# Where partial sums are kept and when a gate's norm is taken: two re-orderings in a hybrid convolution and state-space layer

## The chip, the core and the metric

The kernel runs on one core of a Trainium2 chip. The metric is the device time of one execution in microseconds (us); every kernel is run several times and the median counts. The core has a matrix engine (TensorE, PE in the profile), a vector engine (VectorE, DVE), a scalar engine (ScalarE, ACT), a general engine (GpSimd, POOL) and a queue that starts transfers (SyncE, SP). Each engine takes its own instructions strictly in the order in which they stand, and waits where a semaphore has not come. PE writes its sums to PSUM, from which ACT and DVE read.

## The reference

One layer of a diffusion backbone, on 256 positions of a prompt and 1024 of a sample that share all weights. The part that matters here:

```python
proj = h @ w_in                                  # D = 1024 -> 3072 columns
hc, gb, gc, z, xbc, dtf, dtb = split(proj)
out_a = gb * dwconv1d(gc * hc, w_conv_short)     # short convolution, gated
xbc = silu(dwconv1d(xbc, w_conv_ssd, b_conv_ssd))
dt_f, dt_b = softplus(dtf + dt_bias[0]), softplus(dtb + dt_bias[1])
y = y_f + y_b_rev[:, ::-1] + xh * d_skip         # two chunked scans, chunks of 128
y = rmsnorm(y * silu(z), g_ssd_norm)             # the gate and its norm
out = concatenate([out_a, y]) @ w_out
```

Then follow a second norm and a gated feed-forward block with a 3x3 convolution, which the change does not touch. Everything is in float32.

## The kernel before

A float32 operand is split into two numbers of half the digits, hi and lo, and a product is three matmuls: hi by hi, hi by lo and lo by hi (lines 160, 162 and 164 in `mm3`). Channels lie on the 128 partitions, positions along the free dimension. One **projection** makes 128 columns of `proj` for one set: 8 tiles of the inner dimension by 3 matmuls, so 24 matmuls of 128x256 for the prompt, and 48 of 128x512 for the sample (two chunks of 512).

Each projection loads its weights anew (`wload`, line 146): a transfer, ACT's rounding to hi (line 151), and the subtraction that gives lo (`tt`, line 77), on POOL or on DVE as the caller says (`PG`, `PV`). Every third set of weights goes to the tiles `whx` and `wlx`, of which there is one each; the others to `whi` and `wlo`, of which there are two. So ACT's rounding for a later projection waits until PE is done with the earlier one that used the same tile.

The accumulators are PSUM tiles: `acc` (two of 128x1024), `sa` (three of 128x512) and `yp` (one). `proj_halves` takes an `sa` for the first two projections of the prompt and a whole `acc` for each later one, though a projection of the prompt fills only 256 of its 1024 columns. The counter `s.n` numbers a set's projections from 1.

The prompt's 24 projections run in this order: eight of `xbc` (n = 1 to 8; `i` is 0 to 7; readers ACT at line 396 and two DVE operations at line 80, the convolution), four of `zproj` (z0 to z3, n = 9 to 12; reader ACT at line 409, whose result a transfer of ACT's queue writes away), then `outa` four times (n = 13 to 24). `outa` makes three projections: hc (reader ACT, line 423), gc (reader DVE, a product; then ACT at line 431 and two DVE operations of the convolution), and gb (reader DVE, a product; then ACT at line 440 and a DVE subtraction). Beside them runs `dtstage`, the step sizes: one small matmul (line 458), then a chain that alternates between ACT (lines 461 to 502) and DVE (lines 468 to 498). `dttok` transposes its result on PE (lines 513 and 523; before the last one DVE makes `dg`, line 520).

The sample's projections follow, and then the state-space part. `ssd_pass2` runs over the chunks in units (two to a chunk, one for each group of heads): `front` makes a chunk's transposes and products, `prep` the decay matrices, `output` the 12 or 8 small matmuls of y (line 657), and `fill` puts half a projection of the sample between them. The `gate` of a chunk is a generator of three steps: load z, then multiply and square (ACT and DVE), then the norm: two matmuls by a tile of ones (line 800), ACT's Ln and Exp (lines 804 and 805), and the product on DVE. `post_p` and `post_s` say behind which unit each step is issued. After the last unit the last chunk's norm is issued, and the rest of the fillers; then the gated result is split into hi and lo for the output projection (`mya`, `myb`).

The program's text is not the order on an engine: a scheduler places the instructions by their dependences and priorities, and `after` pins a few behind others. A tile is waited for as a whole: an instruction that writes one part of a tile waits for the readers of its other parts too.

Of the kernel before, what the change touches and what calls it, by code (L numbers as in the profile page):

```python
# [6 lines left out]
F32 = mybir.dt.float32  # L7
F32R = mybir.dt.float32r
AF = mybir.ActivationFunctionType
ALU = mybir.AluOpType  # L10
# [6 lines left out]
TP, TS = 256, 1024  # L17
# [11 lines left out]
TA = TP + RA * GW  # L29
# [26 lines left out]
def body(nc, tc, A):  # L56
    cnt = [0]

    def T(pool, shape, tag, bufs, dt=F32):
        cnt[0] += 1  # L60
        return pool.tile(list(shape), dt, tag=tag, bufs=bufs, name=f"{tag}_{cnt[0]}")
# [7 lines left out]
    def close_pool(g):  # L69
        g.__exit__(None, None, None)  # L70

    act = nc.scalar.activation
# [6 lines left out]
    def stt(out, a, s, b, op0, op1):  # L79
        V.scalar_tensor_tensor(out=out, in0=a, scalar=s, in1=b, op0=op0, op1=op1)  # L80
# [14 lines left out]
    def smv(n):  # L95
        a, b = SMO[n]
        return sm[:, a:b]
# [29 lines left out]
    def pacc():  # L127
        return T(ps, [P, 1024], "acc", 2)
# [4 lines left out]
    def psa():  # L133
        return T(ps, [P, 512], "sa", 3)
# [11 lines left out]
    def wload(src, lo_eng, raw=None):  # L146
        if raw is None:
            raw = T(wst, [P, KT, P], "raw", 2)
        dma(raw, src)
        hi, lo = wpair()  # L150
        act(hi, raw, AF.Copy)  # L151
        tt(lo, raw, hi.bitcast(F32), ALU.subtract, lo_eng)
        return hi, lo

    def mm3(outs, wh, wl, n, ks=None):

        mms = []
        for k in ks or range(n):
            for o, rh, rl in outs:
                nc.tensor.matmul(o, wh[:, k, :], rh(k), start=k == 0, stop=False)  # L160
            for o, rh, rl in outs:
                nc.tensor.matmul(o, wh[:, k, :], rl(k), start=False, stop=False)  # L162
            for o, rh, rl in outs:
                mm = nc.tensor.matmul(o, wl[:, k, :], rh(k), start=False, stop=k == n - 1)  # L164
            mms.append(mm)
        return mms
# [108 lines left out]
    xq = T(xy, [P, 4, TS], "xs", 1)  # L275
# [34 lines left out]
    for k in range(KT):  # L310
# [7 lines left out]
        x = xs[k]  # L318
        tt(x, x, rs, ALU.mult)
        hi = T(hsp, [P, TS], "h", 16, F32R)  # L320
        act(hi, x, AF.Identity, scale=aff[:, 0, k, 1:2], bias=col(0, k, 1))
        ts(x, x, aff[:, 0, k, 1:2], col(0, k, 1), ALU.mult, ALU.add)
        lo = T(hsp, [P, TS], "h", 16, F32R)
# [10 lines left out]
        q, i = k // 4, k % 4  # L334
# [11 lines left out]
    for name, t0, n, v in (("p", 0, TP, 0), ("s", TP, TS, 1)):  # L346
        s = S()
# [11 lines left out]
    def proj(s, m, lo_eng):  # L359
        g = proj_halves(s, m, lo_eng)  # L360
        next(g)
        return next(g)

    def proj_halves(s, m, lo_eng):
        s.n += 1
        wh, wl = wload(A["w_in"][m], lo_eng, T(nrm, [P, KT, P], "x", 8) if s.name == "p" else None)
        pp = psa() if s.name == "p" and s.n <= 2 else pacc()
        outs = []
        for a, b in s.chunks:
            outs.append((pp[:, a:b], (lambda k, a=a, b=b: s.hi(k)[:, a:b]),  # L370
                         (lambda k, a=a, b=b: s.lo(k)[:, a:b])))
        ks = list(range(KT))
        for half in (ks[0:KT // 2], ks[KT // 2:]):
            ends = mm3(outs, wh, wl, KT, half)
            mid_mm[0] = ends[0]
            last_mm.append(ends[-1])
            yield pp[:, 0:s.T]
# [36 lines left out]
    def outa(s, j, lo_eng):  # L414

        n = s.T
        w = [smv("wcs")[:, j * 3 + t:j * 3 + t + 1] for t in range(3)]
        g = proj_halves(s, j, lo_eng)
        next(g)
        yield  # L420
        p1 = next(g)
        u = T(cv, [P, n], "cv", 4)
        act(u, p1, AF.Copy)
        yield
        g = proj_halves(s, 8 + j, lo_eng)
        next(g)
        yield
        p2 = next(g)
        tt(u, p2, u, ALU.mult)
        v = T(cv, [P, n], "cv", 4)  # L430
        act(v, u, AF.Copy, scale=w[1])
        conv1d_sb(v, u, w, n)
        yield
        g = proj_halves(s, 4 + j, lo_eng)
        next(g)
        yield
        p3 = next(g)
        tt(v, p3, v, ALU.mult)
        hi = T(cv, [P, n], "xl", 2, F32R)
        act(hi, v, AF.Copy)  # L440
        lo = T(cv, [P, n], "xl", 2, F32R)
        tt(lo, v, hi.bitcast(F32), ALU.subtract)
        dma(oad[j, 0, :, s.t0:s.t0 + n], hi.bitcast(F32))
        dma(oad[j, 1, :, s.t0:s.t0 + n], lo.bitcast(F32))
        yield
# [59 lines left out]
    def dttok(s, v, e2, ce):  # L505
        s.tok = T(sd, [P, s.nc, 2, 40], f"tok{s.name}", 1)
        for c0 in range(0, s.nc, 4):
            cn = min(4, s.nc - c0)
            tp = psa()
            for c in range(cn):  # L510
                for i, src in enumerate((v, e2)):
                    o = (c * 2 + i) * 40
                    mm = nc.tensor.transpose(tp[:, o:o + 40], src[:, (c0 + c) * L:(c0 + c + 1) * L],
                                             ident[0:40, 0:40])
                    if c0 == c == i == 0:
                        after(mm, last_mm[-1])
            act(s.tok[:, c0:c0 + cn].rearrange("p c i r -> p (c i r)"), tp[:, 0:cn * 80], AF.Copy)
        dg = T(cv, [40, 8, 40], "cv", 4)
        for i in range(s.nc):
            V.tensor_scalar(out=dg[:, i, :], in0=ident[0:40, 0:40], scalar1=ce[:, i:i + 1],  # L520
                            scalar2=None, op0=ALU.mult)
        pdx = psa()
        nc.tensor.matmul(pdx[:, 0:s.nc * 40], ones[0:40, :],
                         dg[:, 0:s.nc].rearrange("p c r -> p (c r)"), start=True, stop=True)
        s.dec = T(sd, [P, s.nc, 40], f"dec{s.name}", 1)
        s.last_exp = act(s.dec.rearrange("p c r -> p (c r)"), pdx[:, 0:s.nc * 40], AF.Exp)
# [164 lines left out]
    xall = T(xy, [P, 4, TP], "xp", 1)  # L691
# [23 lines left out]
    for j in range(4):  # L715
        for _ in outa(SP, j, PG):
            pass
        if j == 0:
            dttok(SP, *dts)
    dts = dtstage(SS, d4_s, silu)  # L720

# [31 lines left out]
    def fillers():  # L753
        for j in range(4):
            yield from zproj_halves(SS, j, PG)
        for j in range(4):
            yield from outa(SS, j, PG)

    filler = fillers()
# [26 lines left out]
    def gate(x, c0, n):  # L786

        z = T(cv, [P, 4, n], "cv", 4)
        for c in range(n // L):
            dma(z[:, :, c * L:(c + 1) * L], zd[c0 + c])  # L790
        yield
        if c0 == 0:
            act(z, z, AF.Silu)
        tt(x, x, z, ALU.mult)
        act(z, x, AF.Square)
        tt(z[:, 0:2], z[:, 0:2], z[:, 2:4], ALU.add)
        yield
        pp = psa()
        for i in range(2):
            mm = nc.tensor.matmul(pp[:, 0:n], ones, z[:, i], start=i == 0, stop=i == 1)  # L800
            if i == 0:
                after(mm, last_mm[-1])
        r = z[:, 2]
        act(r, pp[:, 0:n], AF.Ln, scale=1.0 / 512, bias=epsc)
        act(r, r, AF.Exp, scale=-0.5)
        tt(x, x, r.unsqueeze(1).broadcast_to([P, 4, n]), ALU.mult)
        yield

    gate_p = gate(xall, 0, TP)
    gates = [gate(xq[:, :, c * L:(c + 1) * L], SP.nc + c, L) for c in range(SS.nc)]  # L810
# [5 lines left out]
    def post_s(i):  # L816

        c = i // 2
        if i == 0:
            next(gate_p)  # L820
            next(gates[0])
        if i == 1:
            next(gate_p)
        if i % 2 == 1:
            next(gates[c])
        else:
            if c > 0:
                next(gates[c - 1])
            if c + 1 < SS.nc:
                next(gates[c + 1])  # L830

    ssd_pass2(SP, fill, post_p)
    ssd_pass2(SS, fill, post_s)
    with tc.high_priority():
        next(gates[-1])
    for _ in filler:
        pass
    close_pool(g_sw)
    close_pool(g_sd)

# [2 lines left out]
    g_yb, yb = open_pool("yb")  # L843
    mya = [[T(ya, [P, TA], "ya", 8, F32R) for _ in range(2)] for _ in range(4)]
    myb = [[T(yb, [P, OA], "yb", 8, F32R) for _ in range(2)] for _ in range(4)]
    with tc.high_priority():
        for x, dst, o in ((xall, mya, 0), (xq[:, :, 0:TA - TP], mya, TP), (xq[:, :, TA - TP:], myb, 0)):
            n = x.shape[2]
            for j in range(4):
                g = smv("gsd")[:, j:j + 1]  # L850
                hi, lo = [t[:, o:o + n] for t in dst[j]]
                act(hi, x[:, j], AF.Copy, scale=g)
                stt(lo, x[:, j], g, hi.bitcast(F32), ALU.mult, ALU.subtract)
    close_pool(g_xy)
    close_pool(g_cv)
    close_pool(g_hs)
# [386 lines left out]
```

## Time and profile before

| | |
|---|---|
| time, three runs | 1575.80, 1579.16 and 1581.37 us, median 1579.16 us |
| the profiled execution | 1580.42 us, of which the span on the core is 1578.5 us |
| granted PE clock, mean over the span | 0.991 of full speed |
| instructions of PE, DVE, ACT, POOL | 8722, 1634, 1025, 288 |

The profile is of one execution. "Busy" is the time in which an engine runs an instruction; for PE it includes time at half clock and matmuls that are stretched. A row of a timeline gives start, duration, engine, line and operation, tiles, shape, the count of instructions taken together, and in brackets the idle time ahead and what ended it. A row of a table of windows gives the window, its length, then busy time and instructions of PE, of its weight loads (PEld), of DVE, ACT and POOL, then the granted PE clock, the share of the transfer engines and GB/s. A row of the waits gives the waiting engine, tile and line, who was waited for, and us in all, how often, and the longest.

### The profile page before, as it was taken

What the parts mean: (1) busy time and instruction counts of PE and PEld (TensorE: products, weight loads), DVE (VectorE), ACT (ScalarE), POOL (GpSimd) and SP (SyncE); (2) the same over time, 40 slices, a digit from 0 to 9 for tenths busy, and PEclk for the clock granted to TensorE, in tenths of its full rate; (3) what the DMA queues carried; (4) which work ended last, traced back from release to release, by engine and by line L of the source; (5) the groups of instructions that cost most, each with busy time, mean ns of one, the idle gap of its engine ahead of it and who ended that gap; (6) DMA issues with size and microseconds to landing.
All of it is one profiled execution on the core that took longest, in us unless ns stands there. A gap on an engine that the chain in (4) does not pass through costs nothing. (4 is left out here: it accounts for less than half of the span.)

```text
span 1578.5 us, 22525 instructions
## 1 busy us (share of the span) xinstructions
PE 1525.0 (97%) x8722; PEld 1296.2 (82%) x8722; DVE 1101.3 (70%) x1634; ACT 662.0 (42%) x1025; POOL 513.8 (33%) x288
## 2 busy tenths in 40 slices
PE   6988999999999999999999999999999999999997
PEld 2688667777877888888888888888888888888886
DVE  5665615367787339797666598656679978798696
ACT  6553334257777235443332253332334433433333
POOL 1455001111110001343333333333346555445452
PEclk9999999999999999999999999999999999999999
DMA  8555554343434712322222233212252322343221
GB/s 304 214 184 162 216 202 147 111 150 123 144 101 146 286 67 82 112 73 69 66 68 78 66 133 112 70 65 67 76 184 93 102 99 99 106 161 97 93 78 61
DMA packets 86908, 191.98 MB, mean 122 GB/s; under 512 B 9330, under 2 KB 36626, under 8 KB 86802
## 3 DMA queue, kind: packets, MB, share of 16 engines
q1 hardware_dynamic: 80978, 187.41, 34.6%
q10 hardware_dynamic: 5824, 3.15, 0.7%
q8 instruction: 68, 1.11, 0.3%
q14 instruction: 38, 0.31, 0.1%
HBM read 167.37 MB, written 23.15 MB: 121 GB/s over the span
## 5 line engine op out<-in xcount | busy, mean ns | idle before, releaser
L80 DVE SCALAR_TENSOR_TENSOR cc<-acc,sm,cc 128x504 f32<-128x504 f32 (+5 forms) x836 | 545.7, 665 | 110.8 <-ACT cc L983 52.5
L77 POOL TENSOR_TENSOR wlo<-raw,whi 128x1024 fp32r<-128x1024 f32 (+2 forms) x83 | 193.5, 2331 | 672.4 <-ACT whi L151 518.5
L151 ACT ACTIVATE whi<-raw 128x1024 fp32r<-128x1024 f32 x90 | 95.1, 1057 | 243.6 <-PE acc L162 215.6
L80 DVE SCALAR_TENSOR_TENSOR x<-dn,mod,x 128x288 f32<-128x288 f32 (+2 forms) x176 | 96.1, 546 | 95.3 <-PE dn L164 95.1
L77 POOL TENSOR_TENSOR dlo<-draw,dhi 128x512 fp32r<-128x512 f32 (+1 forms) x88 | 108.9, 1238 | 90.8 <-ACT dhi L1036 88.8
L160 PE MATMUL acc<-ya,whi 128*128 128x512 f32 (+1 forms) x400 | 119.2, 355 | 1.4 <-DVE cv L77 1.4
L162 PE MATMUL acc<-ya,whi 128*128 128x512 f32 (+1 forms) x400 | 119.0, 355 | 0.0
L162 PE MATMUL acc<-oa,whi 128*128 128x512 f32 (+1 forms) x400 | 118.9, 355 | 0.0
L164 PE MATMUL acc<-ya,wlo 128*128 128x512 f32 (+1 forms) x400 | 118.7, 354 | 0.0
L164 PE MATMUL acc<-oa,wlo 128*128 128x512 f32 (+1 forms) x400 | 118.6, 354 | 0.0
L160 PE MATMUL acc<-oa,whi 128*128 128x512 f32 (+1 forms) x400 | 118.4, 353 | 0.0
L160 PE MATMUL dn<-yb,dhi 128*128 128x288 f32 (+2 forms) x352 | 110.0, 313 | 5.3 <-DVE x L80 4.1
L77 POOL TENSOR_TENSOR wlx<-raw,whx 128x1024 fp32r<-128x1024 f32 (+2 forms) x32 | 73.7, 2303 | 120.2 <-ACT whx L151 104.5
L162 PE MATMUL dn<-yb,dhi 128*128 128x288 f32 (+2 forms) x352 | 109.6, 311 | 0.8 <-POOL yb L77 0.8
L164 PE MATMUL dn<-yb,dlo 128*128 128x288 f32 (+2 forms) x352 | 109.6, 311 | 0.0
L160 PE MATMUL acc<-h,whi 128*128 128x512 f32 x320 | 105.7, 407 | 0.0
L1036 ACT ACTIVATE dhi<-draw 128x512 fp32r<-128x512 f32 (+1 forms) x88 | 52.9, 602 | 121.5 <-PE dn L162 50.8
L162 PE MATMUL acc<-h,whi 128*128 128x512 f32 x320 | 101.4, 396 | 0.0
L164 PE MATMUL acc<-h,wlo 128*128 128x512 f32 x320 | 100.8, 396 | 0.0
L160 PE MATMUL dn<-g,dhi 128*128 128x288 f32 (+2 forms) x304 | 95.1, 313 | 0.0
L162 PE MATMUL dn<-g,dhi 128*128 128x288 f32 (+2 forms) x304 | 94.8, 312 | 0.3 <-POOL g L77 0.3
L164 PE MATMUL dn<-g,dlo 128*128 128x288 f32 (+2 forms) x304 | 94.8, 312 | 0.0
(340 smaller groups left out, 3628.9 us busy)
## 6 DMA issues: line engine op xcount, KB each, us to landing
raw<-in_w_up SPq DMA_DIRECT2D x88, 512.0 KB, 3.2
x<-in_w_ada SPq DMA_DIRECT2D x32, 512.0 KB, 5.5
draw<-in_w_down SPq DMA_DIRECT2D x64, 256.0 KB, 2.7
x<-in_w_in SPq DMA_DIRECT2D x24, 512.0 KB, 3.3
raw<-in_w_in SPq DMA_DIRECT2D x22, 512.0 KB, 4.2
xs<-in_w_ad SPq DMA_DIRECT2D x16, 512.0 KB, 8.4
csb<-csds SPq DMA_DIRECT2D x16, 512.0 KB, 3.8
raw<-in_w_out SPq DMA_DIRECT2D x16, 512.0 KB, 3.2
```

What stands on the lines that cost most here:

```text
L77: (eng or V).tensor_tensor(out=out, in0=a, in1=b, op=op)
L80: V.scalar_tensor_tensor(out=out, in0=a, scalar=s, in1=b, op0=op0, op1=op1)
L151: act(hi, raw, AF.Copy)
L160: nc.tensor.matmul(o, wh[:, k, :], rh(k), start=k == 0, stop=False)
L162: nc.tensor.matmul(o, wh[:, k, :], rl(k), start=False, stop=False)
L164: mm = nc.tensor.matmul(o, wl[:, k, :], rh(k), start=False, stop=k == n - 1)
L1036: act(wh, raw, AF.Copy)
```

## The change

Three things. Prompt projections n = 3 and 4 share one `acc`, the second from column 512 on; so do 5 and 6, and so on to 23 and 24. The step sizes' transposes (`dttok`) are issued after the second `outa` and not after the first. And the gate's steps are issued later: a chunk's load and its norm behind odd units in place of even ones, the prompt's in another place, and the last chunk's norm inside the last projection of the sample, with the split of the first part written ahead of it.

```diff
     def proj_halves(s, m, lo_eng):
         s.n += 1
         wh, wl = wload(A["w_in"][m], lo_eng, T(nrm, [P, KT, P], "x", 8) if s.name == "p" else None)
-        pp = psa() if s.name == "p" and s.n <= 2 else pacc()
+        if s.name == "s":
+            pp = pacc()
+        elif s.n <= 2:
+            pp = psa()
+        else:
+            if s.n % 2:
+                s.acc = pacc()
+            pp = s.acc[:, 512 * (1 - s.n % 2):]
...
-        if j == 0:
+        if j == 1:
             dttok(SP, *dts)
...
         if i == 0:
-            next(gate_p)
             next(gates[0])
-        if i == 1:
-            next(gate_p)
         if i % 2 == 1:
             next(gates[c])
-        else:
             if c > 0:
                 next(gates[c - 1])
             if c + 1 < SS.nc:
                 next(gates[c + 1])
+        if i in (0, 3):
+            next(gate_p)
 
     ssd_pass2(SP, fill, post_p)
     ssd_pass2(SS, fill, post_s)
-    with tc.high_priority():
-        next(gates[-1])
-    for _ in filler:
-        pass
...
-    with tc.high_priority():
-        for x, dst, o in ((xall, mya, 0), (xq[:, :, 0:TA - TP], mya, TP), (xq[:, :, TA - TP:], myb, 0)):
-            n = x.shape[2]
-            for j in range(4):
-                g = smv("gsd")[:, j:j + 1]
-                hi, lo = [t[:, o:o + n] for t in dst[j]]
-                act(hi, x[:, j], AF.Copy, scale=g)
-                stt(lo, x[:, j], g, hi.bitcast(F32), ALU.mult, ALU.subtract)
+
+    def split(x, dst, o):
...
+    split(xall, mya, 0)
+    split(xq[:, :, 0:TA - TP], mya, TP)
+    next(filler)
+    next(filler)
+    next(gates[-1])
+    for _ in filler:
+        pass
+    split(xq[:, :, TA - TP:], myb, 0)
```

The new lines move the lines of the kernel behind them by 7 (409 becomes 416, 800 becomes 807).

**Place one: PE, from the prompt's gb0 to its hc1.** Before, the accumulators are `acc_1116` (gb0) and `acc_1168` (hc1); `sa_1149` and `sa_1158` are those of the step sizes' transposes. The 24 matmuls of gb0 stand together, and the transposes behind them:

```order
L162 MATMUL acc_1116<-bc_176,whi_1112 128x256
L164 MATMUL acc_1116<-bc_174,wlo_1113 128x256
L513 MATMUL sa_1149<-cst_66,cv_904 128x40 [waits DVE_49]
L513 MATMUL sa_1149<-cst_66,cv_909 128x40 [waits DVE_49]
L523 MATMUL sa_1158<-cv_1155,ones_70 128x80 [waits DVE_49,PE_49]
L160 MATMUL acc_1168<-bc_173,whx_1164 128x256
L162 MATMUL acc_1168<-bc_175,whx_1164 128x256
L164 MATMUL acc_1168<-bc_173,wlx_1165 128x256 [waits Pool_49]
```

Now gb0 and hc1 share `acc_1110`, and gc1 and gb1 share `acc_1180`; here gb0 ends, five matmuls of gc1 run, and hc1 starts:

```order
L162 MATMUL acc_1110<-bc_176,whi_1106 128x256
L164 MATMUL acc_1110<-bc_174,wlo_1107 128x256
L160 MATMUL acc_1180<-bc_173,whi_1176 128x256 [waits DVE_49,Activation_49]
L162 MATMUL acc_1180<-bc_175,whi_1176 128x256
L164 MATMUL acc_1180<-bc_173,wlo_1177 128x256 [waits Pool_49]
L160 MATMUL acc_1180<-bc_173,whi_1176 128x256
L162 MATMUL acc_1180<-bc_175,whi_1176 128x256
L160 MATMUL acc_1110<-bc_173,whx_1144 128x256 [waits DVE_49]
L162 MATMUL acc_1110<-bc_175,whx_1144 128x256
L164 MATMUL acc_1110<-bc_173,wlx_1145 128x256
```

The transposes are gone from here, and hc1 now waits for DVE, the reader of gb0, since both lie in one tile; five matmuls of gc1 stand in between. All pairs are laid like this: between the two projections of a pair stand the first matmuls of the next pair, 8, 11 and 9 of them behind i2, i4 and i6, none behind z0, 11 behind z2, 4 behind hc0, 5 behind gb0 and gc1, 11 behind hc2, 10 behind gb2 and 5 (of the sample's next projection) behind gc3; the rest of the next pair's first projection follows the second of this pair.

**Place two: ACT, from z2's read to hc0's read.** `whi_1112` are the weights of gb0, `cv_904` and `cv_909` tiles of the step sizes' chain, `xl_1038` is z3. Before:

```order
L410 DMA zd_565<-xl_1004 128x2x128 [waits DMAHW0_49,Activation_49]
L151 ACTIVATE whi_1112<-x_1110 128x1024 [waits DMAHW7_49,PE_49,Pool_49]
L493 ACTIVATE cv_904<-cv_904 40x256 [waits DVE_49]
L409 ACTIVATE xl_1038<-acc_1013 128x256 [waits DMAHW6_49,PE_49]
L410 DMA zd_565<-xl_1038 128x2x128 [waits DMAHW2_49,Activation_49]
L502 ACTIVATE cv_909<-cv_909 40x256 [waits DVE_49]
L151 ACTIVATE whx_1164<-x_1162 128x1024 [waits PE_49,Pool_49]
L423 ACTIVATE cv_1072<-acc_1047 128x256 [waits PE_49]
```

Now (lines 7 further on; `whi_1106` are gb0's weights, `xl_1033` is z3):

```order
L417 DMA zd_565<-xl_1000 128x2x128 [waits DMAHW0_49,Activation_49]
L500 ACTIVATE cv_901<-cv_901 40x256 [waits DVE_49]
L509 ACTIVATE cv_906<-cv_906 40x256 [waits DVE_49]
L151 ACTIVATE whi_1106<-x_1104 128x1024 [waits DMAHW7_49,PE_49,Pool_49]
L416 ACTIVATE xl_1033<-acc_975 128x256 [waits DMAHW6_49,PE_49]
L417 DMA zd_565<-xl_1033 128x2x128 [waits Activation_49]
L430 ACTIVATE cv_1067<-acc_1042 128x256 [waits PE_49]
```

Gb0's weights have moved from ahead of the chain's last two operations on ACT to behind both, and z3's read from between them to behind both.

**Place three: PE, a gate's norm.** Before, a norm stands in an even unit behind the front of the next chunk (`sa_3122` is the front's product) and a few matmuls of the sample's projection (`acc_3153`):

```order
L606 MATMUL sa_3122<-bc_1523,bc_1521 128x128 [waits DVE_49]
L606 MATMUL sa_3122<-bc_1524,bc_1522 128x128
L160 MATMUL acc_3153<-h_225,whi_3149 128x512 x2
L162 MATMUL acc_3153<-h_228,whi_3149 128x512 x2
L164 MATMUL acc_3153<-h_225,wlo_3150 128x512 [waits Pool_49]
L800 MATMUL sa_3139<-cv_2983,ones_70 128x128 [waits DVE_49,Activation_49]
L800 MATMUL sa_3139<-cv_2983,ones_70 128x128
L164 MATMUL acc_3153<-h_225,wlo_3150 128x512
```

Now the same norm's counterpart stands in an odd unit, right behind the matmuls of y (`yp_3235`) and ahead of the sample's projection (`acc_3291`):

```order
L664 MATMUL yp_3235<-wm_3175,xd_3103 64x128
L664 MATMUL yp_3235<-csb_3087,sfw_3008 64x128
L664 MATMUL yp_3235<-csb_3087,sb_3089 64x128
L807 MATMUL sa_3355<-cv_3044,ones_70 128x128 [waits Activation_49]
L807 MATMUL sa_3355<-cv_3044,ones_70 128x128
L160 MATMUL acc_3291<-h_416,whi_3287 128x512 x2
L162 MATMUL acc_3291<-h_419,whi_3287 128x512 x2
```

The norm has moved back by about one unit; it no longer waits for DVE, which makes its squares, but only for ACT, which reads the `sa` tile's earlier content. Before, it stood two units at most behind its squares; the first chunk's and the prompt's now stand together in the fourth unit of the sample.

More of the change, by code (lines that the diff above doesn't have):

```diff
@@ L845, in body @@
     myb = [[T(yb, [P, OA], "yb", 8, F32R) for _ in range(2)] for _ in range(4)]
-    with tc.high_priority():
-        for x, dst, o in ((xall, mya, 0), (xq[:, :, 0:TA - TP], mya, TP), (xq[:, :, TA - TP:], myb, 0)):
-            n = x.shape[2]
-            for j in range(4):
-                g = smv("gsd")[:, j:j + 1]
-                hi, lo = [t[:, o:o + n] for t in dst[j]]
-                act(hi, x[:, j], AF.Copy, scale=g)
-                stt(lo, x[:, j], g, hi.bitcast(F32), ALU.mult, ALU.subtract)
+    def split(x, dst, o):
+        n = x.shape[2]
+        for j in range(4):
+            g = smv("gsd")[:, j:j + 1]
+            hi, lo = [t[:, o:o + n] for t in dst[j]]
+            act(hi, x[:, j], AF.Copy, scale=g)
+            stt(lo, x[:, j], g, hi.bitcast(F32), ALU.mult, ALU.subtract)
+    split(xall, mya, 0)
[6 more added lines that the diff above has]
+    split(xq[:, :, TA - TP:], myb, 0)
     close_pool(g_xy)
```

## The prediction

> **What bounds the kernel now.** I read the head of the page first, then windows laid at the ends of the stages (the prompt's projections from 76 to 158, the sample's to 372, the state-space part to 516, the rest).
>
> ```profile
> span 1578.5 us, 22525 instructions
> PE 1525.0 (97%) x8722; PEld 1296.2 (82%) x8722; DVE 1101.3 (70%) x1634; ACT 662.0 (42%) x1025; POOL 513.8 (33%) x288
> 76.00:158.00 82.00, 73.61 (x580) 70.35 (x579) 49.41 (x65) 41.75 (x61) 44.03 (x18) 0.96 0.54 178
> 372.00:516.00 144.00, 134.92 (x836) 108.66 (x834) 107.35 (x147) 101.74 (x196) 17.60 (x7) 0.98 0.37 124
> 516.00:1578.50 1062.50, 1046.02 (x5878) 924.15 (x5878) 788.16 (x1209) 381.50 (x558) 411.51 (x239) 1.00 0.29 98
> ```
>
> PE is busy 97% of the span and no matmul is removed, so only PE's idle time and half-speed time can change. The change touches the first two stages shown, which leave PE idle for 8.39 and 9.08 us and run at a mean clock of 0.96 and 0.98. The table of PE's waits names who is waited for:
>
> ```profile
> PE sa L800 <- DVE cv L77: 6.4, 4, 3.2
> PE sa L523 <- DVE cv L520: 4.0, 1, 4.0
> PE acc L160 <- ACT xl L409: 3.3, 1, 3.3
> PE acc L160 <- ACT bcp L396: 1.0, 1, 1.0
> PE sa L800 <- ACT btok L540: 0.7, 1, 0.7
> ```
>
> Waits at L800 (a gate's norm) make 7.1 of the 9.08 us of the third stage, and the other three rows 8.3 of the first stage's 8.39. So at most some 15 us of waiting can be won, plus what they do to the clock. That shows in the timeline of PE and in windows of 1 us, whose last columns are PE's clock, the transfers' share and GB/s:
>
> ```profile
> 118.36 0.39 PE L160 MATMUL acc<-bc,whi 128*128 128x256 f32 x1 [3.32 <-ACT xl L409]
> 128.77 0.68 PE L523 MATMUL sa<-cv,ones 40*128 40x80 f32 x2 [3.97 <-DVE cv L520]
> 380.83 1.19 PE L800 MATMUL sa<-cv,ones 128*128 128x128 f32 x4 [3.21 <-DVE cv L77]
> 117.00:118.00 1.00, 0.00 (x0) 0.00 (x0) 0.97 (x3) 0.37 (x2) 0.00 (x0) 1.00 0.00 0
> 127.00:128.00 1.00, 0.00 (x0) 0.00 (x0) 1.00 (x1) 0.00 (x0) 1.00 (x1) 0.55 0.83 233
> 134.00:135.00 1.00, 1.00 (x11) 1.00 (x10) 0.00 (x0) 0.51 (x1) 0.00 (x0) 1.00 0.06 16
> 379.00:380.00 1.00, 0.00 (x0) 0.00 (x0) 1.00 (x4) 0.73 (x2) 0.00 (x0) 0.84 0.28 100
> 387.00:388.00 1.00, 1.00 (x6) 0.83 (x5) 0.90 (x2) 0.57 (x1) 0.00 (x0) 1.00 0.00 0
> 94.35 0.28 PE L160 MATMUL acc<-bc,whx 128*128 128x256 f32 x1
> 94.47 0.28 PE L162 MATMUL acc<-bc,whx 128*128 128x256 f32 x1
> 131.26 0.41 PE L164 MATMUL acc<-bc,wlx 128*128 128x256 f32 x1
> 131.47 0.41 PE L160 MATMUL acc<-bc,whx 128*128 128x256 f32 x1
> ```
>
> The gaps of 3.97 and of 3.21 each let the clock fall to half; it came back by 134 and by 387. The gap of 3.32 ending at 118.36 did not (1.00 at 117). A projection's matmul starts 0.12 after the one ahead of it at full clock and 0.21 at half, so the 5.1 us from 128.77 to about 133.9 hold what 2.7 us would: **2.4 us lost**. From 380.83 to about 386.5 the clock was half too: **2.8 us lost**.
>
> **The gate's norms.** The edit takes the squares (DVE, ACT) two units away from their norm, and the norm's new wait is for ACT's reading of an `sa` tile, done long before. The work that hides it is a unit of y and a half projection of the sample. So the waits at L800 go, 6.4 + 0.7 = 7.1, and with the 3.21 gap its half clock, 2.8: **-10.0**, rounded. Bounds: the 0.7 for ACT may stay and 2.2 more be taken up by other waits of that stage (-7); at best the waits around it shrink too (-10.5). On ACT the two table loads of a norm move from even to odd units, on SP the loads of z move with the steps; neither is ahead of a reader that PE waits for in the order. The last chunk's norm stands within the last projection, and the final readers keep their order on DVE: nothing.
>
> **The step sizes' transposes.** The 3.97 wait goes, and 2.4 of half clock: **-6.4**. The moved instructions are five small matmuls, two reads on ACT and DVE's `dg`; their first user is the state-space part, which begins at about 372 by the windows, so nobody waits. But whether the clock stays up depends on the next part.
>
> **The pairs.** PE now waits, at the second projection of a pair, for the readers of the first, since the tile is waited for whole. How long readers take is in ACT's and DVE's timelines:
>
> ```profile
> 96.86 0.28 PE L160 MATMUL acc<-bc,whi 128*128 128x256 f32 x1
> 97.90 0.55 ACT L396 ACTIVATE bcp<-acc,sm 128x256 f32<-128x256 f32 x1
> 98.48 1.00 DVE L80 SCALAR_TENSOR_TENSOR bcp<-acc,sm,bcp 128x255 f32<-128x255 f32 x2 [2.32 <-ACT bcp L396]
> ```
>
> The projection whose last matmul stands just ahead of 96.86 is read until 99.48: 2.5 us later. Before, the next projection's 24 matmuls (24 x 0.12 = 2.88) covered that, as two whole tiles alternated. Now 8, 11 or 9 matmuls (1.0 to 1.3 us) stand between the halves of a pair, and the third tile's start has 16, 13 or 9 behind the readers that free it. Replaying the order with these durations gives idle time at n5's third matmul 2.2 (POOL's lo stands close behind), n7 1.5, z0 2.0, z1 1.0, hc0 1.0: 7.7. Before, the stretch to hc0's end, from 78.91 to 115.04 (the start at 118.36 less its wait), lasts 36.1 and holds 11 projections (31.7) and about 2.0 of small matmuls, so it loses 2.4. **+5.3**; bounds +2 (each reader half a microsecond sooner) and +8 (nothing overlaps).
>
> **gb0.** Its weights and z3's read now stand on ACT behind both of the step sizes' last operations:
>
> ```profile
> 78.91 0.28 PE L160 MATMUL acc<-bc,whi 128*128 128x256 f32 x1
> 109.15 4.52 DVE L77 TENSOR_TENSOR cv<-cv,cv 40x256 f32<-40x256 f32 x2 [1.23 <-ACT cv L472]
> 117.63 0.42 ACT L493 ACTIVATE cv<-cv 40x256 f32<-40x256 f32 x1 [4.44 <-DVE cv L492]
> 119.61 0.42 ACT L502 ACTIVATE cv<-cv 40x256 f32<-40x256 f32 x1 [1.30 <-DVE cv L77]
> 119.94 1.04 ACT L151 ACTIVATE whx<-x 128x1024 fp32r<-128x1024 f32 x1
> 138.51 2.40 POOL L77 TENSOR_TENSOR wlo<-x,whi 128x1024 fp32r<-128x1024 f32 x1 [0.48 <-ACT whi L151]
> ```
>
> The chain begins some 2 us later, so the second one runs at about 121.9; rounding 1.04 and z3's read end at 123.2, and POOL's lo 2.40 behind the rounding at 125.4. PE, through with hc0 at 120.2, waits 3.1 at gb0's start and 1.9 at its third matmul: 5.0 where 3.32 were. **+1.7**; bounds -1 (the chain no later) and +3. Behind gb0's start all of PE is queued. A gap of 5 us with three matmuls inside is more than the 3.97 that halved the clock; at seven in ten that costs 0.7 x 2.4, **+1.7**, bounds 0 and 2.4.
>
> **outa.** POOL makes every lo here, nearly back to back. DVE's convolution, with both operands in SBUF, takes 1.01 with POOL idle and 2.85 to 3.28 with it running, as it ends behind POOL's operation:
>
> ```profile
> 122.96 3.28 DVE L80 SCALAR_TENSOR_TENSOR cv<-cv,sm,cv 128x255 f32<-128x255 f32 x2 [0.93 <-ACT cv L431]
> 123.41 5.02 POOL L77 TENSOR_TENSOR wlo<-x,whi 128x1024 fp32r<-128x1024 f32 x2
> 138.86 2.85 DVE L80 SCALAR_TENSOR_TENSOR cv<-cv,sm,cv 128x255 f32<-128x255 f32 x2 [0.94 <-ACT cv L431]
> 155.78 1.01 DVE L80 SCALAR_TENSOR_TENSOR cv<-cv,sm,cv 128x255 f32<-128x255 f32 x2 [0.58 <-ACT cv L431]
> ```
>
> The product that frees gb0's half stands on DVE behind that convolution. Take gc0's end as 0. PE runs 20 matmuls of gb0 (2.4), then gc1's: its third waits for rounding (1.05) and POOL (2.40) behind gc0's end, 3.6 with the hops, so 1.1 idle; five are done at 4.1. DVE's convolution starts at 1.6, is held by POOL to 3.6 and, as gb1's lo follows at once, to 6.0; its end 6.4, the product 6.9, hc1 starts at 7.0: 2.9 idle. By the same replay hc2 waits 1.2, gc2 0.25, gc3 1.85, hc3 2.8, gb3 0.3. Sum **+10.4**, where before none of them waited. Bounds: +4 where the convolution finds POOL idle (the row of 1.01, some 1.9 less at hc1, hc3 and partly gc3), and +13 with a half clock more. I take 10.4, since the rows beside busy POOL are two of three.
>
> **Sum.** -10.0 - 6.4 + 5.3 + 1.7 + 1.7 + 10.4 = **+2.7** on the profiled execution's own 1580.42, so 1583; the median of the runs is 1579.16, 1.3 less, so **1582**. About 0.3%, 4.7 us, is what a measurement of this kernel can tell from no change: the forecast is "the same", barely, because the prompt's stage (+12.7, the step sizes' gain counted in) takes what the gates win.
>
> **Rivals.**
>
> *Second halves start at once, or nearly (faster).* If the readers are done in time at most starts, the pairs cost about nothing, the gap at gb0 stays at 3.32 and only -10.0 - 6.4 and perhaps half of the +5.3 are left: about 1579.16 - 14 = 1565. What speaks for it is that the two halves share no column (0 to 255 and 512 to 767), so one could be written while the other is read. The Trainium skill (PSUM — Partial Sum Buffer, "PSUM bank collisions raise a hardware error") says that different engines on different banks run clean, and only the same bank must be guarded; the second half, 2 KiB further on, is another bank by that page, so by its rule no wait is needed and the sum would be this rival's -14; no run shown here has such an overlap. Against it: the program's row of hc1 does wait for DVE, though its weights come from ACT and POOL. It decides when the prompt's stage loses under 5 us. Chance 0.22.
>
> *The clock falls in `outa` too (slower).* The pairs of gaps around hc1 (1.1 + 2.9, five matmuls between) and hc3 (1.85 + 2.8) may each halve the clock: twice 2.4 to 2.8, 5.3 more, so 1587; with the upper bound of gb0, 1590. For it: 3.21 and 3.97 sufficed; against it: 3.32 did not, and here matmuls lie in between. It decides where one gap runs over about 3.2. The Trainium skill (TensorE: Matmul & The Clock Gate, "What's actually happening") has the clock watched in free-running windows of about 3.4 us, one idle window halving it; the rows of 3.21 (halved) and 3.32 (not) fit windows that run free of the gap, though 3.21 is already short of its figure. By it two gaps with matmuls between them would not count as one, and the sum would stay at the forecast's. Chance 0.28.
>
> *The norms wait again.* If squares are late in the odd units too (ACT and DVE are busy 101.74 and 107.35 of 144), the gates win nothing: 1592. The order speaks against it: 0.05.
>
> **Chances and range.** The forecast (1577 to 1586 by itself) has 0.45. The faster rival by itself spans 1560 to 1574 and the clock's 1585 to 1591; the range takes in part of the first and all of the second and leaves out under 2 in 10: 1568 to 1591. Faster by over 0.3% 0.24, within 0.46, slower 0.30.
>
> **What would show it.** Right: no wait of PE for the step sizes' transposes and the norms, the clock at 1.00 around 380, the third stage about 10 us shorter; waits at the projections' matmuls between 83 and 170 of some 23 us in all (7.7 + 5.0 + 10.4), one of about 3 for z3's read and one of about 3 for DVE at hc1; the first stage some 13 us longer. Wrong: few such waits (faster rival), half clock at about 128 to 160 (slower rival), or waits of PE in the third stage that the table of before does not have.

## The result, and the profile after

The changed kernel takes 1592.28 us in the median of six runs (1591.0 to 1595.8), the kernel before 1579.63 us beside it: a ratio of 1.0086, 95% interval 1.0069 to 1.0103. It is 12.7 us slower, where +2.7 was forecast and 1591 was the end of the range. The profiled execution is the slowest of the six, 1595.80 us.

The same windows as before the change, laid at the places of the program that answer to them (the state-space part now ends at 529.0; the columns are those explained above):

```profile
span 1593.8 us, 22522 instructions
PE 1532.7 (96%) x8722; PEld 1304.2 (82%) x8722; DVE 1103.5 (69%) x1634; ACT 662.3 (42%) x1025; POOL 512.0 (32%) x288
```

```profile
76.00:176.40 100.40, 81.71 (x577) 77.20 (x576) 47.84 (x65) 41.80 (x62) 43.07 (x18) 0.88 0.45 148
390.40:529.00 138.60, 132.49 (x837) 108.58 (x836) 109.65 (x146) 103.62 (x196) 19.17 (x7) 0.99 0.38 129
```

The prompt's stage is 18.4 us longer (100.40 for 82.00): 10.3 more of idle PE (18.69 for 8.39) and 8.1 more of busy PE, for about the same 577 matmuls at a mean clock of 0.88 in place of 0.96. The state-space part is 5.4 shorter. That makes +13.0 up to the output projection; it starts at 529.05 where it was 516.12, +12.9, as PE's timelines of the changed kernel and of before show. The rest of the span, 2.3 longer (1064.8 for 1062.5), lies behind that start.

```profile
529.05 0.59 PE L160 MATMUL acc<-ya,whi 128*128 128x256 f32 x2 [3.39 <-DVE cv L77]
516.12 0.59 PE L160 MATMUL acc<-ya,whi 128*128 128x256 f32 x2 [1.41 <-DVE cv L77]
```

PE's table of waits, of the changed kernel, the rows that the change made or left (three columns: us in all, times, longest):

```profile
PE acc L160 <- DVE cv L77: 8.2, 3, 3.4
PE acc L164 <- POOL wlo L77: 5.7, 4, 1.7
PE acc L160 <- ACT xl L416: 3.4, 2, 2.6
PE sa L613 <- DVE wm L77: 2.2, 1, 2.2
PE acc L160 <- DVE bcp L80: 1.8, 1, 1.8
PE acc L164 <- POOL wlx L77: 1.5, 2, 0.8
PE acc L160 <- DVE xp L80: 1.4, 1, 1.4
PE sa L807 <- DVE sfw L77: 0.6, 1, 0.6
```

No row is left for the step sizes' transposes, and the norms (now L807) wait 0.6 for 7.1. In their place stand readers of the other half of a tile (DVE cv, xp and bcp, ACT xl), POOL's lo, and at L613 (a product of `front`) DVE's operation that makes a decay matrix. That matmul's operands are `bc` tiles, which DVE does not make there; by the kernel's text what it waits for is a free `sa` tile, since that DVE operation reads one. The 8.2 of the first row are 2.68 at hc1, 2.10 at hc3 and the 3.39 of the output projection. Where the second half waits longest, at hc1 and hc3, the timelines of PE, DVE and POOL of the changed kernel show who is late:

```profile
138.98 0.58 PE L160 MATMUL acc<-bc,whx 128*128 128x256 f32 x1 [2.68 <-DVE cv L77]
166.05 0.58 PE L160 MATMUL acc<-bc,whx 128*128 128x256 f32 x1 [2.10 <-DVE cv L77]
```

```profile
133.60 4.80 DVE L80 SCALAR_TENSOR_TENSOR cv<-cv,sm,cv 128x255 f32<-128x255 f32 x2 [0.93 <-ACT cv L438]
138.50 0.42 DVE L77 TENSOR_TENSOR cv<-acc,cv 128x256 f32<-128x256 f32 x1
160.69 4.78 DVE L80 SCALAR_TENSOR_TENSOR cv<-cv,sm,cv 128x255 f32<-128x255 f32 x2 [0.93 <-ACT cv L438]
133.25 4.87 POOL L77 TENSOR_TENSOR wlo<-x,whi 128x1024 fp32r<-128x1024 f32 x2 [4.09 <-ACT whi L151]
```

The convolution takes 4.80 us, beside two of POOL's operations that end at 138.12, where it had 1.01 with POOL idle; the product that reads gb0's half comes right behind it, at 138.50, and hc1 starts when it ends. And the clock: windows of PE's half-speed stretches in the prompt's stage of the changed kernel, then the only one of before:

```profile
86.90:90.30 3.40, 3.40 (x18) 3.40 (x18) 0.00 (x0) 0.00 (x0) 0.93 (x1) 0.51 0.70 267
124.40:131.20 6.80, 5.10 (x22) 4.81 (x23) 0.00 (x0) 1.60 (x4) 4.68 (x2) 0.50 0.44 146
138.10:144.90 6.80, 5.92 (x28) 5.92 (x29) 1.15 (x3) 0.96 (x2) 0.02 (x1) 0.51 0.45 139
165.40:172.20 6.80, 6.15 (x29) 6.16 (x30) 0.92 (x3) 1.19 (x2) 0.00 (x0) 0.51 0.42 132
```

```profile
127.20:134.00 6.80, 5.23 (x24) 5.11 (x25) 2.18 (x4) 0.74 (x3) 1.24 (x1) 0.51 0.62 188
```

Such a stretch is 3.4 or 6.8 us long; 3.4 us at half clock is called a half-speed unit below (not to be confused with a unit of `ssd_pass2`), and 6.8 us a double one. PE is busy at half speed for 20.57 us (3.40 + 5.10 + 5.92 + 6.15) where it was for 5.23. Half of the difference is lost: 7.7. With the 10.3 of idle time that is 18.0 of the stage's 18.4.

### The profile page after: what moved, and what is told of

Its sections match the earlier page's. It is cut to its first block, busy times and chain, and to the rows that moved or that the text cites. A ratio compares the mean times of both kernels' runs of the same rounds, so it can differ in the third digit from the quotient of the medians.

```text
span 1593.8 us, 22522 instructions
## 1 busy us (share of the span) xinstructions
PE 1532.7 (96%) x8722; PEld 1304.2 (82%) x8722; DVE 1103.5 (69%) x1634; ACT 662.3 (42%) x1025; POOL 512.0 (32%) x288
```

## The experiments

Theories at the start: **(1)** the pairs are what costs, because the second projection of a pair waits for the readers of the first, in waiting and in half-speed clock behind it; **(2)** the pairs are nearly free and the new places of the gates and of the last norm cost. All kernels but the two of fill run the same matmuls as before.

**One part at a time.** `e1_pairs` is the kernel before with the pairs alone, `e2_gates` with the gates' and the last norm's new places alone, `e3_dttok` with the step sizes' move alone.

```diff
# e1_pairs
-        pp = psa() if s.name == "p" and s.n <= 2 else pacc()
+        if s.name == "s":
+            pp = pacc()
...
+            pp = s.acc[:, 512 * (1 - s.n % 2):]
# e3_dttok
-        if j == 0:
+        if j == 1:
             dttok(SP, *dts)
```

> Only the pairs: prompt projections two to a tile, step sizes and gates as before. Theory (the pairs cost, since the second projection of a pair waits for the readers of the first in the same tile): the prompt's stage, 18.4 us longer with the whole change, is longer by that and by the 4.0 to 6.4 that the step sizes' move had won, so 1598 to 1604 us; PE waits for readers at L160 of some 10 us. Rival (the pairs are nearly free, and the loss comes from the gates' and the last norm's new places): 1585 us or less.

> Only the gates' steps and the last norm inside the last projection; own tiles for each projection of the prompt, step sizes as before. Theory: the waits at the norms go (6 us won up to the last y), the last norm gives 1 to 4 back, so 1574 to 1578 us. Rival: the new places are what costs, 1582 us or more.

> Only the step sizes' transposes one outa later. Theory: the wait of 3.97 at them and two half-clock windows behind it go, 4.0 to 6.4 us, so 1573 to 1576 us. Rival: the matmuls behind them wait for their weights instead, 1579 us.

Measured, against 1581.29 for the kernel before on the same chip: `e1_pairs` 1598.87, ratio 1.0117 (1.0094 to 1.0139); `e2_gates` 1577.06, 0.9974 (0.9961 to 0.9986); `e3_dttok` 1581.43, 1.0000 (0.9987 to 1.0012). So +17.6, -4.2 and +0.1, together +13.5, near the whole change's 12.7: theory 1 holds, theory 2 falls. The profile of `e1_pairs` is of an execution at its median (1597.98), and its prompt's stage shows both parts of the cost with the pairs alone:

```profile
76.00:176.20 100.20, 80.75 (x572) 75.80 (x571) 47.60 (x64) 41.69 (x61) 43.23 (x18) 0.88 0.46 144
```

Against before that is 11.1 more of idle PE and 7.1 more of busy PE, with the same seven half-speed units as in the changed kernel. The step sizes' move, alone, wins nothing, against what I expected. PE's and DVE's timelines of `e3_dttok` say why:

```profile
139.54 0.68 PE L523 MATMUL sa<-cv,ones 40*128 40x80 f32 x2 [3.60 <-DVE cv L520]
```

```profile
134.16 2.84 DVE L80 SCALAR_TENSOR_TENSOR cv<-cv,sm,cv 128x255 f32<-128x255 f32 x2 [0.94 <-ACT cv L431]
137.04 2.35 DVE L520 TENSOR_SCALAR cv<-cst,cep 40x40 f32<-40x40 f32 x2
```

The wait has moved with the transposes: it is 3.60 for 3.97. Its operand `dg` (L520) is put on DVE behind the convolution of whichever `outa` comes just before. In `e1_pairs`, where the transposes keep their old place, PE's table of waits has no row for them at all: by then PE has been held up elsewhere.

**The same room, no shared tile.** `e4_four` is the whole change, but each prompt projection from the third on has one of four tiles of 512 columns.

```diff
...
+    def pacc(s=None):
+        if s is not None and s.name == "p":
+            return T(pc[1], [P, 512], "half", 4)
+        return T(pc[1], [P, 1024], "acc", 2)
...
-            pp = s.acc[:, 512 * (1 - s.n % 2):]
+        pp = psa() if s.name == "p" and s.n <= 2 else pacc(s)
...
+    pc_next("pc2")
     for i in range(8):
         xbc(SP, i, (SP.X + bcp)[i], PG if i % 3 else PV)
...
+    pc_next("pc3")
     dts = dtstage(SS, d4_s, silu)
```

> The whole change, but the prompt's projections from the third on take one of four tiles of 512 columns each, from a pool of their own, in place of two tiles of 1024 shared by two. Same room, no tile with two users. Theory (the wait for the tile as a whole is the cost): no wait for readers at L160 is left in the prompt's stage, the wait for z3's read and the one at i = 4 go too, so the stage is 8 to 11 us shorter than before, and the gates give 3 to 6: 1563 to 1569 us. Rival (readers are late whatever the tile, or POOL's weights bound the stage): 1585 us or more.

Measured 1570.30, ratio 0.9940 (0.9917 to 0.9964) to the kernel before: by the medians some 22 us faster than the changed kernel, with the same PSUM. In its table of PE's waits no reader of an accumulator of the prompt is left, nor the waits of before for z3's read (3.3) and for `bcp` (1.0). What is left in its prompt's stage is 0.3 for ACT's rounding, POOL's lo, 1.9, and the step sizes' transposes, back with 3.8 and the double half-speed stretch behind them:

```profile
PE half L172 <- POOL wlx L77: 1.9, 1, 1.9
PE sa L531 <- DVE cv L528: 3.8, 1, 3.8
PE sa L614 <- DVE wm L77: 2.1, 1, 2.1
PE acc L168 <- DVE cv L77: 3.4, 1, 3.4
```

(Its lines are 8 further on than the changed kernel's in `mm3`, 1 in `dttok` and `front`, and 3 at the norm.) So the cost of the pairs is the tile with two users, not late readers or POOL as such. The time came out 1 us above what I expected; I had left the returning 3.8 out, but no run separates that.

**The last norm, and `dg` earlier.** `e5_four_end` is `e4_four` with the last norm and the split as before the change; `e6_dg_early` is that, with the prompt's `dg` issued in the step sizes' chain.

```diff
# e6_dg_early, in dtstage, behind ce
+        if s.name == "p":
+            s.dg = T(sd, [40, 8, 40], "dgp", 1)
+            for i in range(s.nc):
+                V.tensor_scalar(out=s.dg[:, i, :], in0=ident[0:40, 0:40], scalar1=ce[:, i:i + 1],
+                                scalar2=None, op0=ALU.mult)
...
```

> As e4_four, but the last norm and the split behind it as before the change (the norm ahead of the rest of the last projection, no part of the split between). Theory (the norm inside the last projection makes the output projection wait 3.39 in place of 1.41, for the readers of the last accumulator that stand on DVE behind the norm's work): that wait is 1.4 again, 2.0 won, and up to 1.7 more where the longer gap had let the clock fall for a window: 1566 to 1569 us, against 1570.3 for e4_four. Rival (the norm waits somewhere else instead): 1570 us or more.

> As e5_four_end, and DVE's two operations of line 520 (dg, of the prompt) are issued with the step sizes' chain, right where their operand is ready, ahead of outa's convolutions on DVE. Theory (the matmul of line 523 waits 3.4 to 4.0 because dg stands on DVE behind a convolution that POOL holds, whichever outa it is issued behind): that wait goes, and the half-clock windows behind it, 3.8 + 1.7 to 3.4: 1560 to 1564 us. Rival (the transposes' own inputs, or the weights of the projection behind, are late too): 1566 us or more.

Measured against 1580.67 before: `e5_four_end` 1570.93, 0.9941 (0.9920 to 0.9962), the same as `e4_four`: the theory falls and the rival holds. The wait at the output projection is 1.4 again, but the norm ahead of it waits 1.4 in its turn, as the table of PE's waits of `e5_four_end` shows:

```profile
PE acc L168 <- DVE cv L77: 1.4, 1, 1.4
PE sa L810 <- DVE cv L77: 1.4, 1, 1.4
```

`e6_dg_early`: 1566.83, 0.9913 (0.9897 to 0.9930), 4.1 less than `e5_four_end`. The wait at L523's matmul is gone, and with it the double half-speed stretch; a single unit at 121.5 has come up behind the 1.9 for POOL's lo, and the median missed the 1560 to 1564 expected; by the time alone it lies where the rival was put (1566 or more). The wait for POOL's lo was the same 1.9 in `e5_four_end`, so what came up is the half clock behind it and not a new wait. It is the fastest version here: 13.8 us faster than before, and by the medians some 25 than the changed kernel.

**POOL's part in it.** `e7_lo_dve` is the whole change with the lo weights of the prompt's `outa` made on DVE.

```diff
-        for _ in outa(SP, j, PG):
+        for _ in outa(SP, j, PV):
```

> The whole change, but the weights' lo of the prompt's outa is made on DVE in place of POOL (the scheduler then also puts more of the next pair between two halves, 23 matmuls at hc1 and hc3 in place of 5 and 10). Theory (the second halves wait in outa for a reader that stands behind a convolution held by POOL, and third matmuls for POOL's lo): of the 8.2 us of waits from 134 to 167 two or less are left, and one or two of the half-clock episodes there go: 1579 to 1587 us. Rival (the readers are late by themselves; DVE with the lo on top is later still): 1592 us or more.

Measured 1577.96, ratio 0.9981 (0.9969 to 0.9992) to the kernel before, by the medians some 14 us faster than the changed kernel and 1 us better than expected. PE's timeline from 123 on has three waits left in `outa` and one at the sample's projection behind it, 3.5 us together for the changed kernel's 8.2 (two or less was expected); the last row here is DVE's convolution behind gc1, which takes 1.00 with no operation of POOL beside it:

```profile
128.65 0.39 PE L164 MATMUL acc<-bc,wlo 128*128 128x256 f32 x1 [0.61 <-DVE wlo L77]
135.61 0.39 PE L160 MATMUL acc<-bc,whx 128*128 128x256 f32 x1 [1.18 <-ACT cv L430]
149.51 0.39 PE L164 MATMUL acc<-bc,wlo 128*128 128x256 f32 x1 [0.49 <-DVE wlo L77]
156.52 0.74 PE L160 MATMUL acc<-h,whx 128*128 128x512 f32 x2 [1.24 <-ACT cv L430]
137.14 1.00 DVE L80 SCALAR_TENSOR_TENSOR cv<-cv,sm,cv 128x255 f32<-128x255 f32 x2
```

There is no half-speed stretch between 105 and 415. Since the scheduler also put more of the next pair between the halves, POOL's share and the longer cover aren't told apart here; the two waits for DVE's product are gone by both.

**What the clock costs.** `e8_fill` is the whole change with 76 matmuls that nobody reads, in the three gaps at gb0, hc1 and hc3; `a1_again` is the changed kernel once more, and `fill_again` the same as `e8_fill`, on one chip.

```diff
+        fill_n = {14: 20, 16: 28, 22: 28}.get(s.n, 0) if s.name == "p" else 0
+        if fill_n:
+            pf = psa()
+            for q in range(fill_n):
+                mm = nc.tensor.matmul(pf[:, 0:TP], hp_hi[0][:, q % 4, 0:P], hp_hi[0][:, q % 4],
+                                      start=True, stop=True)
+                after(mm, s.fill if q else last_mm[-1])
+                s.fill = mm
```

> The whole change, and 76 matmuls whose result nobody reads, in an sa tile: 20 ahead of gb0's start, 28 ahead of hc1 and of hc3, where PE waited 2.65, 2.68 and 2.10 us besides shorter waits. Theory (in these places PE only waits, and the gaps let the clock fall three times for two windows of 3.4 us each): the added matmuls cost little beyond the waits that they fill, the three episodes of half clock between 124 and 172 go, and the time falls by 3 to 8: 1584 to 1589 us. Rival (the clock does not matter there, the readers set the pace): 1592 us or more, by what the matmuls add, up to 9.

> The changed kernel once more, for a second profile and beside fill_again on one chip. Its profile so far was its slowest execution. Theory (waits are the same in every execution, and half-clock windows come and go): the same waits of 18.6 us in all between 83 and 170, but fewer half-clock windows there than the seven of the first profile, and a stage that is shorter by 1 to 1.7 us for each. Rival (the clock falls in the same places each time): seven again.

> e8_fill once more, beside a1_again, to bound what the half clock in outa costs. Theory: no half-clock window between 124 and 172, and 2 to 5 us faster than a1_again. Rival (the clock there costs nothing on average): within 1 us of a1_again or slower.

Measured: `e8_fill` 1589.78 (0.8 above the range expected), ratio 1.0063 (1.0046 to 1.0080); `a1_again` 1590.80, 1.0077 (1.0063 to 1.0090); `fill_again` 1588.63, 1.0059 (1.0047 to 1.0071). Windows over the prompt's stage, of `fill_again` and of `a1_again`:

```profile
76.00:175.00 99.00, 88.67 (x688) 82.54 (x687) 52.17 (x72) 48.39 (x69) 43.36 (x18) 1.00 0.51 165
```

```profile
76.00:176.40 100.40, 81.08 (x576) 76.62 (x575) 47.76 (x64) 41.56 (x61) 42.90 (x18) 0.90 0.46 146
```

With more than a hundred more instructions on PE in about the same window, the fill kernel is further on. In the profiles its output projection starts 8.1 us earlier (520.75 for 528.82). But 2.1 of that were there ahead of the first fill, at hc0's third matmul (rows of `fill_again`, then of `a1_again`):

```profile
115.48 0.39 PE L164 MATMUL acc<-bc,wlx 128*128 128x256 f32 x1 [0.76 <-POOL wlx L77]
520.75 0.98 PE L160 MATMUL acc<-ya,whi 128*128 128x256 f32 x2 [3.39 <-DVE cv L77]
```

```profile
117.56 0.39 PE L164 MATMUL acc<-bc,wlx 128*128 128x256 f32 x1 [0.76 <-POOL wlx L77]
528.82 0.59 PE L160 MATMUL acc<-ya,whi 128*128 128x256 f32 x2 [3.39 <-DVE cv L77]
```

Two of the six half-speed units of `a1_again` lie ahead of that place (at 86 and 103), where nothing was filled, and `fill_again` happened to have none there; `e8_fill` has two (at 84 and 101) and a mean clock of 0.97. So some 6 us are gained behind the first fill, where waits are filled with about as much work and the clock stays at 1.00. On the whole time less is seen: the medians differ by 2.2 us, and their intervals overlap. The profiled executions differ by 5.5 (1588.04 and 1593.53), but the one is the fastest of its five and the other the second slowest of its six, and the fill kernel has a double half-speed unit behind the 3.39 wait where `a1_again` has a single one. So the clock's cost in the stage is shown in the profiles, and its worth on the whole time is put at 2 to 5 by these runs, not settled. The half clock as such is no accident of one profile: the clock granted over the whole span, on record for every execution, is 0.986 to 0.991 in `a1_again` (mean 0.988), 0.991 to 0.993 in `fill_again` (0.992) and 0.990 to 0.995 in the kernel before beside them (0.993).

`a1_again` has nearly the same waits as the first profile and six half-speed units in place of seven, as its theory had it. But a unit fewer did not make it 1 to 1.7 us shorter: its output projection starts at 528.82 for 529.05, since half speed loses 0.6 less there (busy for 19.34 us for 20.57) and the waits are 0.8 longer (19.4 for 18.6). Nor do all units come in the same places: a wait of 1.8 at z0 is followed by one in `a1_again` (first pair of rows) and not in the first profile (second pair):

```profile
101.72 0.36 PE L160 MATMUL acc<-bc,whi 128*128 128x256 f32 x1 [1.78 <-DVE bcp L80]
103.20:106.60 3.40, 3.40 (x19) 3.40 (x18) 0.00 (x0) 0.00 (x0) 0.17 (x1) 0.51 0.54 170
101.95 0.36 PE L160 MATMUL acc<-bc,whi 128*128 128x256 f32 x1 [1.79 <-DVE bcp L80]
103.00:106.40 3.40, 3.40 (x31) 3.40 (x30) 0.00 (x0) 0.29 (x1) 0.60 (x1) 1.00 0.61 214
```

**The wait for the decay matrix.** `e9_behind_prep` is `e6_dg_early` with a gate's two products on DVE pinned behind the unit's last operation of `prep`.

```diff
-        tt(x, x, z, ALU.mult)
+        after(V.tensor_tensor(out=x, in0=x, in1=z, op=ALU.mult), prep_last[0])
...
-        tt(x, x, r.unsqueeze(1).broadcast_to([P, 4, n]), ALU.mult)
+        after(V.tensor_tensor(out=x, in0=x, in1=r.unsqueeze(1).broadcast_to([P, 4, n]), op=ALU.mult),
+              prep_last[0])
```

> As e6_dg_early, and a gate's two products on DVE (by z, and by the norm's result) are pinned behind the last DVE operation of the same unit's prep, where before they stood ahead of two of its operations. Theory (of the gates' 7.1 us of waits some come back as a wait of 2.0 to 2.4 at line 606 for a decay matrix, which DVE makes late because two gate products now stand ahead of it in one odd unit): that wait falls under 0.5 and its half-clock window goes, 1562 to 1565 us against 1566.8 for e6_dg_early. Rival (DVE is full there in any order; the wait only changes its name): 1566 us or more.

Measured 1575.32, ratio 0.9972 (0.9960 to 0.9983): by the medians 8.5 slower than `e6_dg_early`. PE's timeline of `e9_behind_prep`:

```profile
385.38 0.71 PE L624 MATMUL sa<-bc,bc 128*128 128x128 f32 x4 [0.44 <-DVE wm L77]
393.74 1.10 PE L569 MATMUL sa<-xd,btok 128*128 128x256 f32 x4 [2.15 <-ACT cv L439]
459.67 0.71 PE L624 MATMUL sa<-bc,bc 128*128 128x128 f32 x4 [0.75 <-DVE wm L77]
487.01 0.99 PE L822 MATMUL sa<-cv,ones 128*128 128x128 f32 x4 [4.55 <-DVE cv L77]
```

The longest wait of PE for the operation that makes the decay matrix (now L624) is 0.75, in another chunk, for 2.4, so the products ahead of it did make it late; but a wait of 2.15 for ACT stands about one unit ahead of that place instead, with a half-speed unit behind it, and the last norm waits 4.55 for DVE. On the time the rival holds.

## Why the prediction was wrong

*The pairs' waits: right, and a little too large.* At n5, n7, z0, z1 and hc0 I replayed 2.2, 1.5, 2.0, 1.0 and 1.0; measured 1.73, 1.38, 1.79, 0.80 and 0.76. At gb0 3.1 and 1.9; measured 2.65 and 1.37. In `outa` 10.4 in seven places; measured 8.16 in five. Sum 23.1 forecast, 18.6 measured. The mechanism at hc1 is as it was told: the convolution, held by two of POOL's operations, then the product, then PE.

*The pairs' clock: the step that failed.* I gave the half clock behind gb0 seven chances in ten, 1.7, and left `outa` at full clock; the slower rival had the two stretches at hc1 and hc3, at 5.3. Both came, and a further one at 86.9 that no case had. The clock's net term was -2.4 + 1.7 = -0.7; the profile has +7.7. My threshold, "where one gap runs over about 3.2", was read from too few rows: half speed stood behind waits of 2.68, 2.65, 2.10 and 1.73, with shorter waits near by. Nor is the length of one wait a threshold at all: that of 1.8 at z0 had half speed behind it in one execution of the changed kernel and not in another. So each of the waits forecast needed a chance of half clock of its own, and only those at gb0 had one. How much of the 7.7 would come back on the whole time at full clock is a second question, and the fill kernels leave it at 2 to 5. The rule of the Trainium skill that I cited (TensorE: Matmul & The Clock Gate, "What's actually happening"), by which an idle window of about 3.4 us halves the clock, does not agree with these rows if idle means wholly idle; the unit of 3.4 us does agree.

*The step sizes: wrong by themselves.* "The 3.97 wait goes" is false for the edit alone (`e3_dttok`). In the whole change it goes, but by the pairs, since it goes in `e1_pairs` without the move too: PE has waited for other things by then.

*The gates: too large.* -10.0 forecast; `e2_gates` shows -4.2, the windows of the changed kernel -5.4 (up to the output projection's start; a half-speed unit of 3.4 us stands behind it). The waits at the norms do go, 7.1 to 0.6. What I had costed at nothing came back: two gate products in one odd unit on DVE make a decay matrix, and with it the release of PE's `sa` tile, late (2.2 at L613, with a half-speed unit behind it), and the last norm inside the last projection makes the output projection wait 3.39 for 1.41. The second is a shift rather than a cost, by `e5_four_end`.

*The faster rival.* "Second halves start at once" is false for this program, as its rows of waits said. But the halves can be kept apart: `e4_four` gives them tiles of their own and runs 1570.30, near the rival's 1565. The rule of the Trainium skill cited there (PSUM — Partial Sum Buffer, "PSUM bank collisions raise a hardware error"), that accesses of different engines to different banks run clean, is in agreement with it: in the profile of `e4_four` DVE reads one `half` tile from 126.65 to 127.07 while PE's matmuls write another at full pace, every 0.12 us.

*The other two rivals.* The slower rival had the mechanism, at 1587 to 1590; the time lies above it mainly because the gates won less. The rival of the norms names 1592, which is the time measured, but by luck: the norms do not wait again (0.6 for 7.1).

In sum, by the profile: waits 3.1 less than forecast (23.1 - 2.4 - 3.3 - 4.0 = +13.4, measured +10.3), the clock 8.4 more, the gates 4.6 less won (-5.4 for -10.0): 2.7 - 3.1 + 8.4 + 4.6 = 12.6. That the medians differ by 12.7 is partly luck, since the profiled executions differ by 15.4 and the sum ends at the output projection. The split is borne out better by `e1_pairs`, profiled at its median: its span is 17.5 us longer than that of before, the prompt's stage 18.2 longer (11.1 of waiting and 7.1 of busy PE), and the state-space part 0.8 shorter.

## What to carry to other kernels

Two users of one tile are two users of one lock: before sharing, ask whether the reader of one part must end before the writer of the other starts, and make tiles of their own where the columns don't overlap. A gap ahead of PE costs its length and may cost as much again behind it at half speed (here 2.68 us at hc1, and half of 5.92 behind it); count both when waits are added, even waits of 2 us. And a wait that "goes" with a moved instruction goes only if its operand is ready at the new place: look for what stands ahead of the operand on its own engine.

## What had not been expected of the hardware

The granted clock moves in units of 3.4 us, one or two at a time (3.40 at 86.9, 6.80 at 124.4, 138.1 and 165.4), and gaps of 1.7 to 2.7 us were followed by half speed, while one of 3.32 before the change was not. The same gap at the same place was, in `e3_dttok`:

```profile
118.32 0.58 PE L160 MATMUL acc<-bc,whi 128*128 128x256 f32 x1 [3.33 <-ACT xl L409]
117.40:124.20 6.80, 5.88 (x27) 5.88 (x28) 2.26 (x7) 2.82 (x6) 2.37 (x1) 0.50 0.35 99
```

The 3.39 wait ahead of the output projection was followed by half speed in some profiles (the changed kernel's, `fill_again`'s) and not in that of `e4_four`. So a wait of one and the same length can go either way; what decides it isn't shown here. DVE's convolution steps, with both operands in SBUF, were held behind POOL's operations: two steps took 4.80 us beside two of POOL's in a row, and 1.00 or 1.01 with POOL idle.
